# Moving the attention's elementwise work off GpSimd in a hybrid decoder layer

## The chip, the cores and the metric

The kernel runs on one core of a Trainium2 chip. The metric is the device time of one execution in microseconds. A core has TensorE (PE, matmuls, with the weight loads shown as PEld), VectorE (DVE), ScalarE (ACT), GpSimd (POOL) and SyncE (SP, which issues DMAs). Each engine runs its instructions in the order in which they were written to it, and waits on semaphores for the others.

## The reference

One layer, 512 tokens, width 1024, all in float32:

```python
x = x + 0.5 * swiglu(rms_norm(x, n1), gate1, up1, down1)          # width 2816
p = rms_norm(x, nm) @ w_in                                        # z | xBC | dt | q | k | v
y = rms_norm(ssd(conv(xBC), dt) * silu(z))                        # 16 heads of 64, chunks of 128 tokens
q, k = rms_norm(q), rms_norm(k)                                   # 8 heads, 2 parts of 64 each
p1, p2 = softmax(mask(q1 @ k1.T / 8)), softmax(mask(q2 @ k2.T / 8))
o = rms_norm((p1 - lam * p2) @ v) * 0.8                           # per head, width 128
x = x + concat(y, o) @ w_out
x = x + 0.5 * swiglu(rms_norm(x, n2), gate2, up2, down2)
```

## The kernel before, in words

TensorE takes its operands as pairs: a high part rounded to the fast float32 form (fp32r) and a low part, the remainder; a product is three matmuls, high by high, high by low, low by high (`mm3`, lines 168 to 172). So each weight tile, after its DMA into `raw`, is split by `split_part` (lines 124 to 129): a cast to `whi`, by ScalarE (line 128) or, while the flag `pool_hi` is set, by GpSimd (line 126), and a difference `wlo` on VectorE (line 129).

The stages follow one another: first feed-forward, projections with convolution and state-space part, attention, output projection, second feed-forward. The attention is the stage of the change. It runs over eight heads `h`, and in each over four blocks `i` of 128 query tokens, block `i` looking at the first (i+1)*128 keys.

- `qk_proj(h)` projects q and k of one head in two halves of 256 tokens (matmuls of lines 603 to 605, tiles `qk_0` and `qk_1`). It is a filler: a generator that `fill()` advances by one block at a time between other work. It runs about two heads ahead. `qk_half` (line 747) then forms the norm of q and k (lines 749 to 752 and `rsqrt_act`, lines 738 to 742), `qf` and `kf` (757, 759), the casts to `qs` and `kh` on ScalarE (766, 769) and the low parts `qs` and `kl` on GpSimd (767, 770).
- `qk_tr(h)` transposes these on TensorE (788) and copies them out (791 on VectorE for `klT`, 793 on ScalarE).
- `att_s(h, i)` makes the scores `sc` of both parts (808 to 810), their maxima `nmx` (813, 814), the exponentials `pe` with their sums `l` on ScalarE (818), and then p1/l1 - lam*p2/l2: reciprocal (820), a factor (821), the scaling of the first part on GpSimd (822) and the fused difference on VectorE (823).
- `att_t(h, i)` transposes the result (831) and splits it into `atH` (ScalarE, 834) and `atL` (VectorE, 835). `att_av(h)` multiplies by v (845 to 847) and takes squares and a scaled copy on ScalarE (850, 851).
- `att_n(h)` is the head's norm: column sums of the squares `om` (857), `v` = mean plus epsilon (860), `y0` = v ** -0.5 from a logarithm and an exponential (861, 862), and one Newton step, o = o*y0 * (1.5 - 0.5*v*y0*y0), whose products are on GpSimd (864, 866 to 868). `o_split` (893, 894) splits the outcome for the output projection.
- `y_split` (line 873, in head 6) loads the state-space part's output again and splits it: cast on GpSimd (880), difference on VectorE (881). From head 6 on, pieces of the output projection (`wo`, lines 170 to 172) are the fillers.

The loop that sets the program order is at lines 944 to 976. On top of it a scheduler with a timing model of its own reorders the instructions of all engines within what data and buffers allow, when the kernel is built. `pool_hi` is set at line 943 and taken back at line 959, at head 6. There are two PSUM buffers for projections (`J`), four for single banks (`M`) and one for the wide scores (`A`); `qs`, `kh`, `kl` and `pe` have three buffers each.

Of the kernel before, what the change touches and what calls it, by code (L numbers as in the profile page):

```python
# [8 lines left out]
F32 = mybir.dt.float32  # L9
# [4 lines left out]
ALU = mybir.AluOpType  # L14
# [4 lines left out]
P = 128  # L19
# [19 lines left out]
def hymba_layer(ctx: ExitStack, tc: tile.TileContext, xT, gu1, dn1, wxbc, wdt, wz, wv, wqk,  # L39
# [7 lines left out]
    psum = {}  # L47

    def psum_open(**bufs):
        """One set of PSUM pools at a time: A tiles take two banks, M and J tiles one."""  # L50
        for cm, _ in reversed(list(psum.values())):
            cm.__exit__(None, None, None)
        psum.clear()
        for tag, n in bufs.items():
            cm = tc.tile_pool(name=f"ps{tag}", bufs=n, space=PSUM)
            psum[tag] = (cm, cm.__enter__())
# [14 lines left out]
        return psum["P"][1].tile([P, T], F32, tag="P", name=name)  # L71

    def ffn_plan(parts, early):
        """Order of the work: a part's products with w_down run between the next part's with gate and up."""
        plan, downs, f = [], [], 0
        for pi, n in enumerate(parts):
            if pi == 0:
                plan += [("std", e, g) for e in range(n) for g in range(2)]
            else:
                for c in range(n):  # L80
                    if pi == 1 and c == 0:
                        plan += downs[:early]
                        downs = downs[early:]
                    plan.append(("seven", f + c // 2 * 2, c % 2))
                    while downs and len(downs) > KD * (n - 1 - c) // n:
                        plan.append(downs.pop(0))
            downs = [("down", pi, d) for d in range(KD)]
            f += n
        return plan + downs
# [84 lines left out]
    xpool_cm = tc.tile_pool(name="x1", bufs=1, side="right")  # L174
    xpool = xpool_cm.__enter__()
    x1 = [xpool.tile([P, T], F32, name=f"x1_{d}") for d in range(KD)]
    # products of zeros while the first loads run: the tensor engine's clock is up when the data comes
    zeros = const.tile([P, T], BF16, name="zeros")
    V.memset(zeros, 0.0)
    warm = pP("warm")  # L180
# [24 lines left out]
    xnpool = xn_cm.__enter__()  # L205

    def rsqrt(dst, v, shape, tag):
        """dst = v ** -0.5 for small tiles: exponent-halving start and Newton steps."""
        y = tiny.tile(shape, F32, tag=f"rs_y{tag}", name="rs_y")
        t = tiny.tile(shape, F32, tag=f"rs_t{tag}", name="rs_t")  # L210
        ti = t.bitcast(I32)
        V.tensor_scalar(ti, v.bitcast(I32), 1, None, op0=ALU.arith_shift_right)
        V.tensor_scalar(y.bitcast(I32), ti, -1, 0x5F3759DF, op0=ALU.mult, op1=ALU.add)
        for it in range(3):
            V.tensor_mul(t, y, y)
            V.scalar_tensor_tensor(t, t, -0.5, v, op0=ALU.mult, op1=ALU.mult)
            V.scalar_tensor_tensor(dst if it == 2 else y, t, 1.5, y, op0=ALU.add, op1=ALU.mult)

    class Normed:
        """x * w in two parts, and the factors 1/rms(x) by token (columns, and a row on all partitions)."""  # L220

        def __init__(self, pool, sqp, wcol, name):
            self.sqp, self.pool = sqp, pool
# [61 lines left out]
    prep(4)  # L285

    def ffn(xn, x, done, name, parts, early):
        """x += 0.5 * swiglu(xn).

        The 128-column tiles of gate and up in the first part take the products as they are. The others take them in  # L290
        pairs, in Winograd's form of Strassen's product of 2x2 blocks (halves of the contraction, of the tokens
        and the two tiles), seven block products in place of eight, on the normalized tokens.
        """
        sp_cm = tc.tile_pool(name=f"str{name}", bufs=1)
        hp_cm = tc.tile_pool(name=f"ffn{name}", bufs=5)
        sp, hp = sp_cm.__enter__(), hp_cm.__enter__()
# [1 line left out]
        al = sp.tile([P, 4, 7, 256], F32R, name=f"al{name}")  # L298

        def operands(i):  # L300
            # 0: A12, 1: A22, 2: S1, 3: S2, 4: S3, 5: S4, 6: A11, 7: A21
            tx = hp.tile([P, 8, 256], F32, tag="hp", name="tx")
            for k, at in ((i, 6), (i + 4, 0)):
                c = xn.wcol + k
                V.scalar_tensor_tensor(tx[:, at:at + 2, :].rearrange("p a b -> p (a b)"), x[k], col[:, c:c + 1],
                                       xn.rbc, op0=ALU.mult, op1=ALU.mult)
            V.tensor_add(tx[:, 2], tx[:, 7], tx[:, 1])
            V.tensor_sub(tx[:, 3], tx[:, 2], tx[:, 6])
            V.tensor_sub(tx[:, 4], tx[:, 6], tx[:, 7])
            V.tensor_sub(tx[:, 5], tx[:, 0], tx[:, 3])  # L310
            S.copy(ah[:, i], tx[:, 0:7])
            V.tensor_sub(al[:, i], tx[:, 0:7], ah[:, i].bitcast(F32))

        def h_pair(g, u):
            """silu(g) * u in two parts; g and u: the two tiles, [P, 2, T]."""
            h = hp.tile([P, 2, 2, T], F32R, tag="hp", name="h")
            S.activation(g, g, AF.Silu)
            V.tensor_mul(u, u, g)
            S.copy(h[:, 0], u)
            V.tensor_sub(h[:, 1], u, h[:, 0].bitcast(F32))  # L320
            return h
# [6 lines left out]
                PE.matmul(ps, lhsT=lo, rhs=ah[:, i, a], start=False, stop=i == 3)  # L328

        def seven(c, u, nm_):  # L330
            """c[:, f, t] = the pair's two tiles by the two halves of the tokens."""
            w = piece(1)
            q = [pP(f"{nm_}{z}") for z in range(4)]
            half = lambda z, b: q[z][:, b * 256:(b + 1) * 256]
            cc = c.rearrange("p f (t b) -> p f t b", t=2)
            c1, u2, u3, u4 = (u[:, z] for z in range(4))
            product(half(0, 0), 6, w[0], 0)
            product(half(0, 1), 0, w[0], 512)
            S.copy(c1, half(0, 0))
            V.tensor_add(cc[:, 0, 0], half(0, 1), c1)  # L340
            product(half(1, 0), 2, w[1], 0)
            product(half(1, 1), 4, w[1], 512)
            product(half(2, 0), 3, w[2], 0)
            V.tensor_add(u2, half(2, 0), c1)
            V.tensor_add(u3, half(1, 1), u2)
            V.tensor_add(cc[:, 1, 1], half(1, 0), u3)
            V.tensor_add(u4, half(1, 0), u2)
            product(half(2, 1), 1, w[2], 512)
            V.scalar_tensor_tensor(cc[:, 0, 1], half(2, 1), -1.0, u3, op0=ALU.mult, op1=ALU.add)
            product(half(3, 0), 5, w[3], 0)  # L350
            V.tensor_add(cc[:, 1, 0], half(3, 0), u4)
# [56 lines left out]
        hp_cm.__exit__(None, None, None)  # L408
        sp_cm.__exit__(None, None, None)

# [1 line left out]
    xsave = dram.tile([KD, P, T], F32, name="xsave")  # L412
    nm = [None]

# [8 lines left out]
    xpool_cm.__exit__(None, None, None)  # L423
    psum_open(A=2, M=2, J=2)

# [1 line left out]
    mix_cm = tc.tile_pool(name="mix", bufs=1)  # L427
    mix = mix_cm.__enter__()
    row = mix.tile([P, NROW], F32, name="row")
# [158 lines left out]
    V.tensor_scalar(e2, nm.v, EPS, None, op0=ALU.mult)  # L588

    def tok_proj(name, cb, ahead=2):  # L590
        """Projection onto 256 columns by token blocks; yields after each block's matmuls."""
        ws = [piece(ahead), piece(ahead)]
        for half in range(2):
            ps = pJ(f"{name}_{half}")
# [135 lines left out]
            pass  # L730
    last_ssd = lambda: drain_c(8)

# [1 line left out]
    def rsqrt_act(dst, v, shape):  # L734
        """dst = v ** -0.5: exp(-ln(v) / 2) and a Newton step."""
        y = tiny.tile(shape, F32, tag="ra_y", name="ra_y")
        t = tiny.tile(shape, F32, tag="ra_t", name="ra_t")
        S.activation(y, v, AF.Ln)
# [8 lines left out]
    def qk_half(h, half, ps):  # L747
# [16 lines left out]
        kh = at.tile([P, 4, 2, 64], F32R, tag="kh", name="kh", bufs=3)  # L764
        kl = at.tile([P, 4, 2, 64], F32R, tag="kl", name="kl", bufs=3)
        S.copy(qs[:, :, 0, :], qf)
        G.tensor_sub(qs[:, :, 1, :], qf, qs[:, :, 0, :].bitcast(F32))
        kd = kf.unsqueeze(2).to_broadcast([P, 4, 2, 64])
        S.copy(kh, kd)
        G.tensor_tensor(kl, kd, kh.bitcast(F32), op=ALU.subtract)  # L770
        qk[h].append((rs, qs, kh, kl))

    qk = {}
# [25 lines left out]
    def att_s(h, i):  # L799
# [19 lines left out]
                         accum_out=l[:, t:t + 1])  # L819
        V.reciprocal(l, l)  # L820
        V.scalar_tensor_tensor(l[:, 1:2], l[:, 1:2], -1.0, lam, op0=ALU.mult, op1=ALU.mult)
        G.tensor_scalar(pe[:, 0, :K], pe[:, 0, :K], l[:, 0:1], 1.0, op0=ALU.mult, op1=ALU.mult)
        V.scalar_tensor_tensor(pe[:, 0, :K], pe[:, 1, :K], l[:, 1:2], pe[:, 0, :K], op0=ALU.mult, op1=ALU.add)  # L823
        sm[h, i] = pe

# [28 lines left out]
    def att_n(h):  # L854
# [6 lines left out]
        S.activation(y0, v, AF.Ln)  # L861
        S.activation(y0, y0, AF.Exp, scale=-0.5)
        o = oT[:, h, :]
        G.tensor_mul(o, o, y0)
        S.activation(y0, y0, AF.Square)
        G.tensor_mul(v, v, y0)
        G.tensor_scalar(v, v, -0.5, 1.5, op0=ALU.mult, op1=ALU.add)
        G.tensor_mul(o, o, v)

    # output projection pieces that fill the tensor engine while the last head's attention runs  # L870
    yhl = []

    def y_split():
        yh = xnpool.tile([P, KD, T], F32R, tag="xnh", name="yh")
        yl = xnpool.tile([P, KD, T], F32R, tag="xnl", name="yl")
        for t in range(0, KD, 2):
            yt = wpool.tile([P, 1024], F32, tag="raw", name="yt", bufs=3)
            nc.sync.dma_start(yt, ysave[:, t:t + 2].rearrange("p a b c -> p (a b c)"))
            h = yh[:, t:t + 2, :].rearrange("p a b -> p (a b)")
            G.tensor_scalar(h, yt, 1.0, 1.0, op0=ALU.mult, op1=ALU.mult)  # L880
            V.tensor_sub(yl[:, t:t + 2, :].rearrange("p a b -> p (a b)"), yt, h.bitcast(F32))
        yhl.extend((yh, yl))

# [56 lines left out]
    fillers += [qk_proj(h) for h in range(1, 8)]  # L940
    fill()
    fill()
    pool_hi[0] = True
    for h in range(8):
        qk_tr(h)
        fill()
# [9 lines left out]
        prep(taken[0] + 1)  # L956
        fill()
        if h == 6:
            pool_hi[0] = False
            y_split()  # L960
            wo_ps[0], wo_ps[1] = pJ("wo0"), pJ("wo1")
            fillers += wo_fill(0)
# [52 lines left out]
    xn_cm.__exit__(None, None, None)  # L1015
    psum_open(P=8)

# [1 line left out]
    def done2(d):  # L1019
        nc.sync.dma_start(out[d], x2[d])  # L1020

# [62 lines left out]
```

## Time and profile before

| what | value |
|---|---|
| median of three runs | 1207.35 us (1206.51 to 1207.97) |
| span of the profiled execution, first to last instruction | 1203.1 us |
| TensorE busy | 1163.4 us (97%) |
| VectorE busy | 926.0 us (77%) |
| ScalarE busy | 533.8 us (44%) |
| GpSimd busy | 210.6 us (18%) |
| mean granted TensorE clock | 0.990 |

The profile page gives no device time for the profiled execution beside its span; the median of the runs is 4.25 us above it. Busy times are of the union of an engine's instructions. An instruction's duration can overlap that of the next one on the same engine. A matmul's duration is that of its passage through a pipeline, so matmuls overlap and their durations do not add up to TensorE's time.

### The profile page before, as it was taken

What the parts mean: (1) busy time and instruction counts of PE and PEld (TensorE: products, weight loads), DVE (VectorE), ACT (ScalarE), POOL (GpSimd) and SP (SyncE); (2) the same over time, 40 slices, a digit from 0 to 9 for tenths busy, and PEclk for the clock granted to TensorE, in tenths of its full rate; (3) what the DMA queues carried; (4) which work ended last, traced back from release to release, by engine and by line L of the source; (5) the groups of instructions that cost most, each with busy time, mean ns of one, the idle gap of its engine ahead of it and who ended that gap; (6) DMA issues with size and microseconds to landing.
All of it is one profiled execution on the core that took longest, in us unless ns stands there. A gap on an engine that the chain in (4) does not pass through costs nothing.

```text
span 1203.1 us, 19035 instructions
## 1 busy us (share of the span) xinstructions
PE 1163.4 (97%) x7483; PEld 1036.3 (86%) x7483; DVE 926.0 (77%) x1593; ACT 533.8 (44%) x863; POOL 210.6 (18%) x214
## 2 busy tenths in 40 slices
PE   8999999999989999798999998899999999999998
PEld 6889999999967788797998886688789999999997
DVE  6988787787585867989588989636499988787862
ACT  5534343433352355343366675735244443434331
POOL 1000000000031004443255756315100000000000
PEclk9999999999998999899999999999999999999999
DMA  7223333333353224242321102216312333333332
GB/s 231 86 75 97 110 110 97 99 107 88 97 193 114 77 82 140 81 131 73 105 71 36 58 32 76 75 44 209 98 62 89 109 121 100 101 107 102 96 114 83
DMA packets 42393, 119.56 MB, mean 99 GB/s; under 512 B 4608, under 2 KB 9920, under 8 KB 42304
## 3 DMA queue, kind: packets, MB, share of 16 engines
q1 hardware_dynamic: 41024, 114.15, 30.3%
q0 software_dynamic: 1280, 4.20, 1.0%
q8 instruction: 59, 0.97, 0.3%
q14 instruction: 30, 0.25, 0.1%
HBM read 112.00 MB, written 6.32 MB: 98 GB/s over the span
## 4 chain that ended last, share of the span: by engine, by line
PE 40%; DVE 10%; issue 2%; ACT 2%; POOL 1%; DMA 0%; DVEq 0%; ACTq 0%; POOLq 0%
PE s L327 5%; PE s L326 5%; PE s L328 5%; PE dn L170 3%; PE dn L172 3%; PE dn L171 3%; PE wo L170 2%; PE wo L171 2%; PE wo L172 2%; DVE nmx L813 2%; DVE pe L823 1%; PE gu L170 1%; PE gu L172 1%; PE gu L171 1%; DVE wlo L129 1%
## 5 line engine op out<-in xcount | busy, mean ns | idle before, releaser
L129 DVE TENSOR_TENSOR wlo<-raw,whi 128x1024 fp32r<-128x1024 f32 (+3 forms) x225 | 225.9, 1007 | 120.0 <-ACT whi L128 104.4
L128 ACT CAST whi<-raw 128x1024 fp32r<-128x1024 f32 (+2 forms) x204 | 175.7, 865 | 310.2 <-PE s L327 121.7
L327 PE MATMUL s<-al,whi 128*128 128x256 f32 x952 | 265.2, 280 | 0.0
L326 PE MATMUL s<-ah,whi 128*128 128x256 f32 x952 | 263.6, 279 | 0.0
L328 PE MATMUL s<-ah,wlo 128*128 128x256 f32 x952 | 262.6, 279 | 0.0
L327 PEld LDWEIGHTS s<-al,whi 128*128 128x128 f32 x952 | 178.7, 188 | 2.1
L326 PEld LDWEIGHTS s<-ah,whi 128*128 128x128 f32 x952 | 178.5, 188 | 2.0
L328 PEld LDWEIGHTS s<-ah,wlo 128*128 128x128 f32 x952 | 177.2, 187 | 0.1
L170 PE MATMUL dn<-h,whi 128*128 128x512 f32 x352 | 137.6, 394 | 0.0
L172 PE MATMUL dn<-h,wlo 128*128 128x512 f32 x352 | 137.5, 392 | 0.0
L171 PE MATMUL dn<-h,whi 128*128 128x512 f32 x352 | 136.9, 389 | 0.0
L128 ACT CAST whi<-tw 128x1024 fp32r<-128x1024 f32 x68 | 70.3, 1049 | 141.2 <-PE s L327 65.7
L129 DVE TENSOR_TENSOR wlo<-tw,whi 128x1024 fp32r<-128x1024 f32 x68 | 82.1, 1220 | 2.8 <-ACT whi L128 2.5
L172 PEld LDWEIGHTS dn<-h,wlo 128*128 128x128 f32 x352 | 66.1, 188 | 14.6
L171 PEld LDWEIGHTS dn<-h,whi 128*128 128x128 f32 x352 | 66.1, 188 | 12.7
L170 PEld LDWEIGHTS dn<-h,whi 128*128 128x128 f32 x352 | 66.1, 188 | 12.2
L603 PE MATMUL qk<-whi,xhm 128*128 128x256 f32 x256 | 73.3, 287 | 1.1 <-DVE l L820 1.1
L605 PE MATMUL qk<-whi,xlm 128*128 128x256 f32 x256 | 72.8, 285 | 0.0
L604 PE MATMUL qk<-wlo,xhm 128*128 128x256 f32 x256 | 72.7, 284 | 0.0
L362 DVE SCALAR_TENSOR_TENSOR x<-dn,x 128x512 f32<-128x512 f32 x64 | 44.0, 688 | 35.4 <-PE dn L172 34.9
L170 PE MATMUL gu<-xh,whi 128*128 128x512 f32 x160 | 64.9, 406 | 2.7 <-POOL whi L126 1.7
L419 POOL DMA_DIRECT2D xsave<-x x8 | 4.6, 578 | 337.3 <-DVE x L362 337.3
(293 smaller groups left out, 2650.8 us busy)
## 6 DMA issues: line engine op xcount, KB each, us to landing
raw<-in_gu SPq DMA_DIRECT2D x86, 512.0 KB, 3.6
raw<-in_dn SPq DMA_DIRECT2D x48, 384.0 KB, 3.2
raw<-in_wqk SPq DMA_DIRECT2D x16, 512.0 KB, 3.6
raw<-in_wxbc SPq DMA_DIRECT2D x12, 512.0 KB, 3.5
raw<-in_wo SPq DMA_DIRECT2D x10, 512.0 KB, 4.1
raw<-in_dn SPq DMA_DIRECT2D x16, 256.0 KB, 2.7
raw<-in_wz SPq DMA_DIRECT2D x8, 512.0 KB, 3.5
ab<-acs_d SPq DMA_DIRECT2D x8, 512.0 KB, 4.1
```

The lines of the kernel that those rows point to most:

```text
L128: S.copy(hi[:, a:b], raw[:, a:b])
L129: V.tensor_sub(lo[:, a:b], raw[:, a:b], hi[:, a:b].bitcast(F32))
L170: PE.matmul(ps, lhsT=hi, rhs=xh, start=start, stop=False)
L171: PE.matmul(ps, lhsT=hi, rhs=xl, start=False, stop=False)
L172: PE.matmul(ps, lhsT=lo, rhs=xh, start=False, stop=stop)
L326: PE.matmul(ps, lhsT=hi, rhs=ah[:, i, a], start=i == 0, stop=False)
L327: PE.matmul(ps, lhsT=hi, rhs=al[:, i, a], start=False, stop=False)
L328: PE.matmul(ps, lhsT=lo, rhs=ah[:, i, a], start=False, stop=i == 3)
L362: V.scalar_tensor_tensor(x[d], ps, 0.5, x[d], op0=ALU.mult, op1=ALU.add)
L603: PE.matmul(o, lhsT=xh, rhs=hi, start=k == 0, stop=False)
L604: PE.matmul(o, lhsT=xh, rhs=lo, start=False, stop=False)
L605: PE.matmul(o, lhsT=xl, rhs=hi, start=False, stop=k == KD - 1)
```

## The change

In the attention GpSimd's elementwise instructions go to other engines. The low parts of q and k and the scaling of the first softmax part go to VectorE, the casts of the weights (heads 0 to 5) and of y go to ScalarE. The head's norm is written in another way: y0*(1.5 - 0.5*v*y0*y0) is formed first, with two fused instructions on VectorE, and multiplied into o once. Comments were taken out of the file as well, which moves line numbers little: lines 767 to 868 keep theirs.

```diff
@@ qk_half
-        G.tensor_sub(qs[:, :, 1, :], qf, qs[:, :, 0, :].bitcast(F32))
+        V.tensor_sub(qs[:, :, 1, :], qf, qs[:, :, 0, :].bitcast(F32))
...
-        G.tensor_tensor(kl, kd, kh.bitcast(F32), op=ALU.subtract)
+        V.tensor_tensor(kl, kd, kh.bitcast(F32), op=ALU.subtract)
@@ att_s
-        G.tensor_scalar(pe[:, 0, :K], pe[:, 0, :K], l[:, 0:1], 1.0, op0=ALU.mult, op1=ALU.mult)
+        V.tensor_scalar(pe[:, 0, :K], pe[:, 0, :K], l[:, 0:1], None, op0=ALU.mult)
@@ att_n
-        G.tensor_mul(o, o, y0)
-        S.activation(y0, y0, AF.Square)
-        G.tensor_mul(v, v, y0)
-        G.tensor_scalar(v, v, -0.5, 1.5, op0=ALU.mult, op1=ALU.add)
-        G.tensor_mul(o, o, v)
+        t = at.tile([P, T], F32, tag="sq", name="ot")
+        S.activation(t, y0, AF.Square)
+        V.scalar_tensor_tensor(t, t, -0.5, v, op0=ALU.mult, op1=ALU.mult)
+        V.scalar_tensor_tensor(t, t, 1.5, y0, op0=ALU.add, op1=ALU.mult)
+        V.tensor_mul(o, o, t)
@@ y_split
-            G.tensor_scalar(h, yt, 1.0, 1.0, op0=ALU.mult, op1=ALU.mult)
+            S.copy(h, yt)
@@ the loop over heads
-    pool_hi[0] = True
     for h in range(8):
...
         if h == 6:
-            pool_hi[0] = False
             y_split()
```

The scheduler then orders all engines anew. On TensorE, in head 2, before: the transposes of the head's k (khT_6532 and klT_6539, the high and the low part of one of its two halves) with matmuls of head 4's projection (qk_0_6756) between them.

```order
L788 MATMUL khT_6532<-identr,kh 128x128 x4
L605 MATMUL qk_0_6756<-whi,xlm 128x256
L603 MATMUL qk_0_6756<-whi,xhm 128x256
L604 MATMUL qk_0_6756<-wlo,xhm 128x256
L605 MATMUL qk_0_6756<-whi,xlm 128x256
L603 MATMUL qk_0_6756<-whi,xhm 128x256
L604 MATMUL qk_0_6756<-wlo,xhm 128x256
L605 MATMUL qk_0_6756<-whi,xlm 128x256
L603 MATMUL qk_0_6756<-whi,xhm 128x256
L604 MATMUL qk_0_6756<-wlo,xhm 128x256
L605 MATMUL qk_0_6756<-whi,xlm 128x256
L788 MATMUL klT_6539<-identr,kl 128x128 x4
```

The same place on TensorE after the change, up to head 2's scores sc_6719; at_6592 is a transposed softmax tile of head 1.

```order
L788 MATMUL khT_6532<-identr,kh 128x128 x4
L788 MATMUL klT_6539<-identr,kl 128x128 x4
L788 MATMUL qT_6546<-identr,qs 128x128 x4
L788 MATMUL khT_6553<-identr,kh 128x128 x4
L788 MATMUL klT_6560<-identr,kl 128x128 x4
L831 MATMUL at_6592<-ident,pe 128x128 x3
L808 MATMUL sc_6719<-khT,qT 128x384
L809 MATMUL sc_6719<-klT,qT 128x384
```

The projection's matmuls are gone from between; qk_0_6756 starts after head 1's product with v. On VectorE, before: from the maximum of head 1's last scores (sc_6459) to the difference of its two softmax parts (L823).

```order
L813 TENSOR_REDUCE nmx<-sc_6459 128x2
L752 SCALAR_TENSOR_TENSOR qss<-qss,e_4158 128x8
L835 TENSOR_TENSOR atL<-at_6454,atH 128x2x128
L814 TENSOR_TENSOR nmx<-nmx,qrs 128x2
L791 CAST klT<-klT_6539 128x512
L820 RECIPROCAL l<-l 128x2
L740 TENSOR_TENSOR ra_t<-ra_y 128x8
L821 SCALAR_TENSOR_TENSOR l<-l,lam 128x1
L791 CAST klT<-klT_6560 128x512
L741 SCALAR_TENSOR_TENSOR ra_t<-ra_t,qss 128x8
L823 SCALAR_TENSOR_TENSOR pe<-pe,l 128x512
```

The same on VectorE after the change; `ot` and `oT` are head 0's norm.

```order
L813 TENSOR_REDUCE nmx<-sc_6459 128x2
L791 CAST klT<-klT_6539 128x512
L791 CAST klT<-klT_6560 128x512
L814 TENSOR_TENSOR nmx<-nmx,qrs 128x2
L866 SCALAR_TENSOR_TENSOR ot<-ot,ov 128x512
L835 TENSOR_TENSOR atL<-at_6592,atH 128x3x128
L867 SCALAR_TENSOR_TENSOR ot<-ot,osq 128x512
L820 RECIPROCAL l<-l 128x2
L868 TENSOR_TENSOR oT<-oT,ot 128x512
L821 SCALAR_TENSOR_TENSOR l<-l,lam 128x1
L822 TENSOR_SCALAR pe<-pe,l 128x512
L823 SCALAR_TENSOR_TENSOR pe<-pe,l 128x512
```

The norm's three instructions and the scaling now stand in this queue, and the small norm instructions of a projection (L740, L741) are no longer there at this place.

## Rows read from the trace of the kernel before

**Rows 1.** Windows: stretch, length, busy us of each engine (instructions), granted clock, DMA share, GB/s.

```profile
600.00:645.00 45.00, 45.00 (x379) 42.33 (x378) 38.86 (x90) 27.84 (x75) 25.96 (x25) 1.00 0.18 60
645.00:667.70 22.70, 21.32 (x170) 19.27 (x170) 19.64 (x44) 15.14 (x41) 14.84 (x14) 1.00 0.16 47
667.70:690.00 22.30, 22.07 (x182) 20.25 (x180) 20.44 (x43) 16.13 (x43) 15.18 (x15) 1.00 0.16 48
690.00:712.00 22.00, 19.95 (x156) 17.76 (x155) 18.94 (x44) 14.51 (x39) 13.44 (x13) 1.00 0.16 50
712.00:734.00 22.00, 19.94 (x155) 17.39 (x153) 19.35 (x42) 15.67 (x43) 14.06 (x15) 1.00 0.00 1
734.00:760.00 26.00, 23.07 (x118) 18.28 (x119) 23.51 (x37) 14.22 (x33) 12.58 (x11) 1.00 0.47 140
760.00:780.00 20.00, 16.57 (x93) 12.56 (x92) 14.01 (x35) 16.57 (x42) 7.78 (x9) 0.91 0.13 43
```

**Rows 2.** Waits of VectorE, 645 to 734 us: us in total, times, longest.

```profile
DVE l L820 <- ACT pe L818: 6.1, 6, 1.3
DVE pe L823 <- POOL pe L822: 1.7, 4, 0.7
```

**Rows 3.** Timeline of VectorE, 669 to 676 us: start, us, instruction.

```profile
669.05 0.15 DVE L814 TENSOR_TENSOR nmx<-nmx,qrs 128x2 f32<-128x2 f32 x1
669.12 0.68 DVE L791 CAST klT<-klT 128x512 fp32r<-128x512 f32 x1
...
673.38 1.24 DVE L742 SCALAR_TENSOR_TENSOR qrs<-ra_t,ra_y 128x8 f32<-128x8 f32 x1
```

**Rows 4.** Timeline of GpSimd in the same stretch.

```profile
673.05 1.54 POOL L866 TENSOR_TENSOR ov<-ov,osq 128x512 f32<-128x512 f32 x1 [0.28 <-ACT osq L865]
```

**Rows 5.** Lines of VectorE, 592 to 790 us: busy us, mean ns | idle before.

```profile
L823 DVE SCALAR_TENSOR_TENSOR pe<-pe,l 128x256 f32<-128x256 f32 x8 | 9.7, 1206 | 1.1 <-POOL pe L822 0.9
L823 DVE SCALAR_TENSOR_TENSOR pe<-pe,l 128x512 f32<-128x512 f32 x8 | 9.6, 1194 | 2.1 <-POOL pe L822 2.1
L823 DVE SCALAR_TENSOR_TENSOR pe<-pe,l 128x384 f32<-128x384 f32 x8 | 9.4, 1174 | 1.5 <-POOL pe L822 1.5
L821 DVE SCALAR_TENSOR_TENSOR l<-l,lam 128x1 f32<-128x1 f32 x32 | 8.0, 249 | 0.4
...
L742 DVE SCALAR_TENSOR_TENSOR qrs<-ra_t,ra_y 128x8 f32<-128x8 f32 x16 | 7.0, 437 | 0.3
...
L814 DVE TENSOR_TENSOR nmx<-nmx,qrs 128x2 f32<-128x2 f32 x32 | 6.6, 213 | 0.1
...
L752 DVE SCALAR_TENSOR_TENSOR qss<-qss,e 128x8 f32<-128x8 f32 x16 | 6.2, 390 | 0.0
...
L741 DVE SCALAR_TENSOR_TENSOR ra_t<-ra_t,qss 128x8 f32<-128x8 f32 x16 | 5.3, 329 | 0.2
...
L835 DVE TENSOR_TENSOR atL<-at,atH 128x384 fp32r<-128x384 f32 x8 | 4.4, 549 | 0.2 <-ACT atH L834 0.2
...
L740 DVE TENSOR_TENSOR ra_t<-ra_y 128x8 f32<-128x8 f32 x16 | 3.7, 233 | 0.4 <-ACT ra_y L739 0.4
```

**Rows 6.** Lines of VectorE over the whole span, other stages, for prices.

```profile
L387 DVE TENSOR_TENSOR gu<-gu,rbc 128x512 f32<-128x512 f32 x20 | 13.0, 686 | 6.0 <-PE gu L172 6.0
...
L305 DVE SCALAR_TENSOR_TENSOR tx<-x,col,rbc 128x512 f32<-128x512 f32 x16 | 10.8, 748 | 0.0
...
L480 DVE TENSOR_SCALAR a<-u,col 128x512 f32<-128x512 f32 x12 | 6.3, 544 | 2.9 <-ACT xst L487 2.9
...
L310 DVE TENSOR_TENSOR tx<-tx 128x256 f32<-128x256 f32 x8 | 3.0, 424 | 0.0
```

**Rows 7.** Single lines: shortest/median/longest in ns, first and last start.

```profile
L645 DVE TENSOR_SCALAR ab<-ab,acs x64: 269/276/2466, 455.6 to 541.6; 128x128 f32<-128x128 f32 x64
...
L742 DVE SCALAR_TENSOR_TENSOR qrs<-ra_t,ra_y x16: 154/167/1237, 598.3 to 744.3; 128x8 f32<-128x8 f32 x16
```

**Rows 8.** Lines of ScalarE, 592 to 790 us.

```profile
L128 ACT CAST whi<-raw 128x1024 fp32r<-128x1024 f32 x5 | 5.2, 1047 | 8.6 <-DMA raw<-in_wo 6.6 <-PE wo L171 1.8
```

**Rows 9.** Lines of GpSimd, 592 to 790 us.

```profile
L770 POOL TENSOR_TENSOR kl<-kf,kh 128x512 fp32r<-128x512 f32 x16 | 23.4, 1461 | 7.4 <-ACT kh L769 5.1 <-issue 2.3
```

## The prediction

> **What bounds the kernel now.** I read first the windows of the trace around the attention, then the waits of VectorE there, then single instructions of VectorE and GpSimd side by side, and last the prices by line. The first heads keep TensorE full: 45.0 of 45 us. From 645 us on, one head takes about 22.3 us, and TensorE is idle for 1.4, 0.2, 2.1 and 2.1 us of the four stretches, 5.8 us together; in the last two heads it is idle for 2.9 and 3.4 us more [rows 1]. So TensorE is the bound with little room: everything that a better attention can give back is 12.1 us between 645 and 780, and some 1.8 us for the 0.91 of the clock granted in the last stretch. VectorE stands close behind it, busy for 19.6, 20.4, 18.9 and 19.4 us of the same four stretches, mean 19.6; ScalarE has 15.4 and GpSimd 14.4 [rows 1]. What VectorE does not work it waits mainly for the exponentials, 6.1 us, and 1.7 us for GpSimd's scaling of a probability tile [rows 2].
>
> Part of VectorE's busy time is no work. A product of 128x8 elements took 1.24 us from 673.38 us [rows 3], and GpSimd's two-operand product ran from 673.05 to 674.59 us [rows 4]: VectorE's ended when GpSimd's had. The shortest of the same line took 0.154 us [rows 7]. So the two engines hold each other up here, and the change has a gain of its own besides the moved work.
>
> **What the change takes from VectorE.** The extra time by rows, mean less undisturbed price, for eight heads [rows 5 to 7]: the difference of the two softmaxes (L823) 8 x (1.206 - 0.424) + 8 x (1.174 - 0.549) + 8 x (1.194 - 0.748) = 6.3 + 5.0 + 3.6 = 14.8 us. The small ones at 0.15 us each: L821 32 x 0.10, L742 16 x 0.29, L752 16 x 0.24, L741 16 x 0.18, L814 32 x 0.06, L740 16 x 0.08 = 3.2 + 4.6 + 3.8 + 2.9 + 1.9 + 1.3 = 17.7 us. Together 32.5 us, 4.1 us a head. Not all need come back: some may have been idle time otherwise. I take all of it.
>
> **What it adds to VectorE.** qs: 16 x 0.424 = 6.8 us. kl: 16 x 0.686 = 11.0 us. The scaling of the probabilities (L822), 128 to 512 columns: the rows of two other products with a column show 0.276 and 0.544 us for the ends [rows 6, 7], 0.37 and 0.45 us between them, 1.64 us a head, 13.1 us (from both sides: not below the 0.15 us of a tiny instruction, 4.8 us in all, and not above the 0.69 us of a two-operand one at full width, 22 us). The norm: two fused instructions at 0.748 and a product at 0.686, 2.18 us a head, 17.5 us. Sum 48.4 us, 6.1 us a head. Instructions that follow at once overlap: one started at 669.05 for 0.15 us and the next at 669.12 [rows 3], some 0.08 us of overlap, so the 11 new ones of a head cost 0.9 us less: 5.2 us. Net on VectorE: +1.1 us a head (with the overlap uncounted +2.0; with L822 at its low end about 0).
>
> Of the scaling the rows show 0.544 us at 512 columns, against 0.686 us for a two-operand product [rows 6]. The Trainium skill (VectorE: DVE Perf Modes, section The perf-mode tier table) lets a float32 product with a column run at twice the rate of a two-operand one, 1227 against 2293 ns at 2048 columns. The row does not reach that factor. By the page the widest scaling would be 0.37 us, an estimate as 0.686 x 1227 / 2293, all of them 8.9 us in place of 13.1, and the net 0.5 us a head smaller; I keep the row.
>
> **What it adds to ScalarE.** 13 weight casts leave GpSimd, two to a head at 1.05 us [rows 8], and four casts of y in head 6: ScalarE goes from 15.4 to 17.5 us a head, still under VectorE and TensorE; I cost it at nothing as long as the exponentials don't queue behind the casts (a rival below). In the last two heads the weight casts were on ScalarE already.
>
> **What the new order does.** VectorE at 19.6 + 1.1 = 20.7 us, with the 2.6 us a head that it still has to stand idle (22.2 less 19.6), makes a head of 23.3 us in place of 22.2, since nothing in the change takes the wait for the exponentials away. The 1.7 us of waits for GpSimd in four heads go, 0.4 us a head, so I take +0.8 us a head. For five heads (1 to 5) that is +4 us. Head 0 has slack on VectorE (38.9 of 45 us in the first stretch, [rows 1]), and the last two heads have projections of the output to run beside them; there I take nothing, with -6 to +6 us.
>
> Once, a stretch comes without filler. In the order before, as its rows on TensorE show, the transposes of head 2 stand between matmuls of a projection. In the order after, from the last product of head 0's attention to that of head 1's no projection matmul stands on TensorE; the two halves of head 3's projection have already run. Behind the last scores of head 1 (sc_6459) TensorE has 45 matmuls of its own; at 22.3 us for 170 to 182 of them [rows 1], 0.13 us each, that is 5.9 us. VectorE in the same place has 19 instructions from the maximum of sc_6459 to the low part of tile 3: nine of 512 columns (three fused ones at 0.748, six at 0.686), 6.4 us; the maximum over 1024, 1.3 us; 0.55 us for 384 columns, 0.54 us for the scaling, 0.85 us for two of 256 columns, 0.9 us for the tiny ones: 10.5 us, less 18 x 0.08 us of overlap, 9.1 us. TensorE waits for the end of it, as its next product reads that low part: 3.2 us, and with one wait for the exponentials of about 1 us, 4 us.
>
> **The sum.** +4 (five heads) + 4 (the stretch without filler) + 0 (the last two heads) = +8 us. The profiled execution spans 1203.1 us; the median of the runs is 1207.35 us, 4.25 us above the span, which is what lies around it and the spread between executions. Neither is changed by the edit, so I add to the median: 1215 us.
>
> **Rivals.** First, faster: VectorE, freed, keeps ahead of TensorE, and the shorter chains (two hand-overs to GpSimd fewer for each probability tile) let the idle time of TensorE shrink. For it speak the 1.24 us product and the 1.2 us differences [rows 3, 5], and that the order is written by a scheduler which sees instructions undisturbed. It decides if the added work overlaps so well that VectorE has under 19.6 us a head. It gives back at most the 12.1 us of idle time; about 7 of it, 1200 us. Against it: the moved work by rows is larger than what is freed.
> The Trainium skill (GPSIMD Engine Reference, section Elementwise, side-by-side cycle accounting) has VectorE about twice as fast as GpSimd on two-operand work; the rows agree (kl takes 1.46 us on GpSimd [rows 9], and 0.69 us is the price here), and a reader who goes by it alone would forecast this rival.
>
> Second, no difference: the +1.1 us and the two hand-overs cancel, and the stretch without filler is made up in the last heads, where TensorE is idle for 6.4 us: 1207 us.
>
> Third, much slower: ScalarE's queue decides. Two casts of 1.05 us a head stand ahead of exponentials and of the copies that VectorE waits for; if each delays the chain fully in the six heads that get them, 12.6 us come on top of the 4 us of the stretch without filler: 1224 us. Against it: ScalarE has 6.8 us a head free.
>
> **How the numbers follow.** What a measurement of this kernel can tell from no change is about 0.2%, 2.4 us. The forecast, +8 us, has a chance of 0.40; faster 0.27; no difference 0.18; much slower 0.15. So faster 0.27, same 0.18, slower 0.55. Cases of both signs hold much of the chance: the likeliest one's own range is 1210 to 1221 us. The range that should hold 8 times in 10 goes to the faster rival's middle at the low end, 1200, and to the much slower one at the high end, 1224.
>
> **What would show it.** Right: in the profile after, L823 at 0.35 to 0.75 us and L742 near 0.17 us; VectorE busy for over 20 us of a head; TensorE idle for 3 us or more in head 1 or 2, just ahead of its product with V; the period of a head at 23 us. Wrong: a period at or under 22 us, or VectorE under 19.5 us a head (then the moved work is cheaper than its rows say), or long waits of VectorE for ScalarE's casts, which would be the third rival.

## The result, and the profile after

The changed kernel takes 1214.86 us, the median of 4 runs (1213.43 to 1216.13); the kernel before, run beside it, 1206.93 us (1206.06 to 1207.97). The ratio is 1.0065, with a 95% interval of 1.0051 to 1.0079: slower by 8 us. The profiled execution spans 1211.7 us, 8.6 us more than before, at a mean granted clock of 0.982 against 0.990 (the profiled execution of before is a quick one, see below the table of all runs). GpSimd's busy time falls from 210.6 to 90.9 us.

The windows of after around the attention, in the columns of [rows 1].

```profile
600.00:645.00 45.00, 43.47 (x363) 39.67 (x361) 36.39 (x95) 31.36 (x75) 0.00 (x0) 1.00 0.22 71
645.00:667.70 22.70, 19.10 (x127) 16.96 (x128) 18.65 (x55) 15.81 (x41) 0.00 (x0) 0.85 0.00 1
667.70:690.00 22.30, 19.47 (x141) 17.54 (x140) 19.19 (x53) 16.62 (x41) 0.00 (x0) 0.92 0.15 48
690.00:712.00 22.00, 22.00 (x181) 20.48 (x180) 18.62 (x53) 17.59 (x43) 0.00 (x0) 1.00 0.15 48
712.00:734.00 22.00, 20.03 (x156) 17.61 (x155) 19.30 (x53) 16.98 (x43) 0.00 (x0) 1.00 0.08 25
734.00:760.00 26.00, 18.79 (x119) 15.92 (x118) 23.52 (x57) 20.07 (x46) 0.00 (x0) 0.76 0.34 112
760.00:780.00 20.00, 20.00 (x114) 16.28 (x113) 12.94 (x23) 9.94 (x20) 0.00 (x0) 0.96 0.14 40
```

VectorE has more instructions (55, 53, 53, 53 against 44, 43, 44, 42 in the four stretches from 645 us) and is busy for 18.9 us of a stretch on average, against 19.6. That does not mean less work: the stretches are fixed times, and a slower kernel gets less done in each. From the first transposes of q and k (L788) to the second feed-forward, where both kernels have the same stage to do, VectorE is busy for 3.1 us more, and stands idle for 5.6 us more (before, then after):

```profile
598.80:854.40 255.60, 242.66 (x1578) 208.64 (x1577) 190.43 (x373) 152.31 (x360) 129.52 (x124) 0.99 0.25 78
598.70:863.10 264.40, 246.39 (x1570) 212.41 (x1568) 193.64 (x457) 168.18 (x373) 14.50 (x14) 0.95 0.23 75
```

Of TensorE's idle time after, 3.6, 2.8 and 7.2 us lie in three stretches (645 to 667.7, 667.7 to 690, 734 to 760), and in these the granted clock is 0.85, 0.92 and 0.76; the 0.96 of the last stretch is the end of the same time at half clock. Before, it was 1.00 everywhere but in the last stretch.

Lines of VectorE after, 592 to 790 us, that answer to [rows 5]:

```profile
L770 DVE TENSOR_TENSOR kl<-kf,kh 128x512 fp32r<-128x512 f32 x16 | 11.0, 687 | 1.3 <-ACT kh L769 1.1
L767 DVE TENSOR_TENSOR qs<-qf,qs 128x256 fp32r<-128x256 f32 x16 | 6.7, 419 | 0.0
L823 DVE SCALAR_TENSOR_TENSOR pe<-pe,l 128x512 f32<-128x512 f32 x7 | 5.2, 749 | 0.2
...
L867 DVE SCALAR_TENSOR_TENSOR ot<-ot,osq 128x512 f32<-128x512 f32 x7 | 4.8, 689 | 0.1
...
L823 DVE SCALAR_TENSOR_TENSOR pe<-pe,l 128x256 f32<-128x256 f32 x8 | 3.9, 484 | 0.1
L822 DVE TENSOR_SCALAR pe<-pe,l 128x512 f32<-128x512 f32 x7 | 3.4, 479 | 0.0
...
L742 DVE SCALAR_TENSOR_TENSOR qrs<-ra_t,ra_y 128x8 f32<-128x8 f32 x16 | 2.6, 164 | 0.2
```

With no GpSimd instruction from 645 to 780 us the hold-ups are gone: L823 at 256 columns takes 484 ns where it took 1206, L742 164 where it took 437.

What TensorE waits for after, 590 to 780 us (total, times, longest):

```profile
PE o L846 <- DVE atL L835: 5.8, 3, 2.8
PE at L831 <- ACT osq L850: 3.4, 1, 3.4
PE sc L808 <- ACT pe L818: 2.9, 1, 2.9
```

Before, the longest single wait there was this one:

```profile
PE at L831 <- DVE l L821: 1.8, 1, 1.8
```

Now the first of the three places on TensorE's timeline (start, duration, what ended the idle time before it):

```profile
647.72 0.44 PE L808 MATMUL sc<-khT,qT 128*128 128x384 f32 x1 [2.90 <-ACT pe L818]
...
649.76 1.11 PE L831 MATMUL at<-ident,pe 128*128 128x128 f32 x4 [0.88 <-DVE pe L823]
...
653.77 0.63 PE L846 MATMUL o<-atL,vh 128*128 128x512 f32 x1
654.20 0.63 PE L847 MATMUL o<-atH,vl 128*128 128x512 f32 x1
```

The wide scores wait for the one PSUM buffer `A`, which head 1's exponentials still read. There is no projection matmul to run meanwhile. Behind the wait matmuls of 512 columns start 0.43 us apart (653.77 and 654.20) where they start 0.23 us apart at full rate: the clock is at its 1.2 GHz level for 6.8 us. The second place is the product of head 2 with v, on TensorE and then on VectorE:

```profile
675.05 0.49 PE L845 MATMUL o<-atH,vh 128*128 128x512 f32 x1
678.36 0.50 PE L846 MATMUL o<-atL,vh 128*128 128x512 f32 x1 [2.83 <-DVE atL L835]
```

```profile
673.42 1.22 DVE L129 TENSOR_TENSOR wlo<-raw,whi 128x1024 fp32r<-128x1024 f32 x1
...
674.63 1.22 DVE L129 TENSOR_TENSOR wlo<-raw,whi 128x1024 fp32r<-128x1024 f32 x1
675.77 0.42 DVE L813 TENSOR_REDUCE nmx<-sc 128x2 f32<-128x256 f32 x1
676.10 0.68 DVE L751 TENSOR_REDUCE qss<-sqk 128x8 f32<-128x512 f32 x1
676.70 0.42 DVE L767 TENSOR_TENSOR qs<-qf,qs 128x256 fp32r<-128x256 f32 x1
677.03 0.68 DVE L813 TENSOR_REDUCE nmx<-sc 128x2 f32<-128x512 f32 x1
677.63 0.68 DVE L835 TENSOR_TENSOR atL<-at,atH 128x512 fp32r<-128x512 f32 x1
```

VectorE never pauses, but the one instruction that TensorE needs, L835, stands behind a weight split, the projection's norm (L751, L767) and two maxima. `atH` of this tile was written by 675.0 us. In the order of its queue VectorE first serves work that TensorE does not need yet.

The third place is heads 5 and 6, where ScalarE, too, has its queue in the wrong order:

```profile
746.07 0.22 ACT L739 ACTIVATE ra_y<-ra_y 128x8 f32<-128x8 f32 x1
748.40 1.05 ACT L880 CAST yh<-yt 128x1024 fp32r<-128x1024 f32 x1 [2.11 <-DMA yt<-ysave]
...
754.41 0.62 ACT L128 CAST whi<-raw 128x512 fp32r<-128x512 f32 x1 [1.01 <-DMA raw<-in_wo]
754.94 0.61 ACT L893 CAST oh<-oT 128x512 fp32r<-128x512 f32 x1
755.46 0.59 ACT L850 ACTIVATE osq<-o 128x512 f32<-128x512 f32 x1
```

ScalarE stands 2.11 us for the load of a y tile and 1.01 us for a weight; the squares L850, for which TensorE waits 3.4 us, come after; the product that they read had ended by 752.8 us.

### The profile page after: what moved, and what is told of

Same layout as the page of the kernel before. It is cut to its first block, busy times and chain, and to the rows that moved or that the text cites. A ratio compares the mean times of both kernels' runs of the same rounds, so it can differ in the third digit from the quotient of the medians.

```text
span 1211.7 us, 18948 instructions
## 1 busy us (share of the span) xinstructions
PE 1168.3 (96%) x7483; PEld 1040.7 (86%) x7483; DVE 928.9 (77%) x1681; ACT 553.5 (46%) x880; POOL 90.9 (8%) x101
## 4 chain that ended last, share of the span: by engine, by line
PE 50%; DVE 3%; ACT 2%; issue 0%; DMA 0%
PE s L327 5%; PE s L326 5%; PE s L328 5%; PE dn L170 3%; PE dn L172 3%; PE dn L171 3%; PE wo L170 2%; PE wo L171 2%; PE wo L172 2%; PE qk L603 2%; PE qk L604 2%; PE qk L605 2%; PE gu L170 1%; PE gu L172 1%; PE gu L171 1%; PE sc L808 1%
## 5 line engine op out<-in xcount | busy, mean ns | idle before, releaser
L128 ACT CAST whi<-raw 128x1024 fp32r<-128x1024 f32 (+2 forms) x217 | 190.0, 879 | 303.4 <-PE s L327 121.7
L129 DVE TENSOR_TENSOR wlo<-raw,whi 128x1024 fp32r<-128x1024 f32 (+3 forms) x225 | 222.6, 992 | 114.5 <-ACT whi L128 108.6
L172 PE MATMUL dn<-h,wlo 128*128 128x512 f32 x352 | 137.5, 392 | 0.0
L129 DVE TENSOR_TENSOR wlo<-tw,whi 128x1024 fp32r<-128x1024 f32 x68 | 82.0, 1220 | 3.1 <-ACT whi L128 3.0
L172 PEld LDWEIGHTS dn<-h,wlo 128*128 128x128 f32 x352 | 66.1, 188 | 14.6
L172 PE MATMUL gu<-xh,wlo 128*128 128x512 f32 x160 | 63.0, 394 | 0.0
```

What stands on the lines that cost most here:

```text
L128: S.copy(hi[:, a:b], raw[:, a:b])
L129: V.tensor_sub(lo[:, a:b], raw[:, a:b], hi[:, a:b].bitcast(F32))
L172: PE.matmul(ps, lhsT=lo, rhs=xh, start=False, stop=stop)
```

## The experiments

Each of the 12 was timed in five rounds beside the kernel before, in three sets; the kernel before had 1207.1, 1206.4 and 1207.4 us in them. Four ideas were under test. VectorE theory: its added work lengthens each head (the prediction's step of +4 us for five heads). Buffer theory: the norm's new tile `ot` shares the single buffer "sq" with the squares of q and k, and this ties the norm to the projections. Order theory: TensorE waits where the new order leaves no projection matmuls between those of the attention, whatever engine has how much work. ScalarE theory: its casts stand ahead of exponentials and squares.

**Buffer alone, on the kernel before.** No work moves; the square of the norm only goes to the shared buffer.

```diff
-        S.activation(y0, y0, AF.Square)
-        G.tensor_mul(v, v, y0)
+        t = at.tile([P, T], F32, tag="sq", name="ot")
+        S.activation(t, y0, AF.Square)
+        G.tensor_mul(v, v, t)
```

> The kernel before with one thing changed: the square in the head's norm is written to a tile of its own name in the buffer 'sq', of which there is one and in which the squares of the projections' norms stand as well, as in the changed kernel. No instruction moves to another engine. Theory BUFFER (the changed norm's new tile makes a projection's first step wait for the norm of a head, so TensorE runs out of projection matmuls): a run of about 67 matmuls without filler in head 2, slower than before by 4 to 10 us. Theory VECTORE (on record: the added work on VectorE makes a head longer): the same time as before, within 2 us.

Measured 1217.38 us, ratio 1.0086 (1.0072 to 1.0099): 10 us slower for a buffer, at the top of buffer theory's range. TensorE idles 8.3 of 22.7 us and gets a clock of 0.76 in one stretch of that kernel:

```profile
645.00:667.70 22.70, 14.38 (x64) 11.01 (x63) 16.88 (x42) 15.18 (x41) 13.78 (x16) 0.76 0.07 23
```

So the buffer is enough by itself. Is it needed?

**The changed kernel with the norm in place**, without the shared buffer, in four VectorE instructions:

```diff
-        t = at.tile([P, T], F32, tag="sq", name="ot")
-        S.activation(t, y0, AF.Square)
-        V.scalar_tensor_tensor(t, t, -0.5, v, op0=ALU.mult, op1=ALU.mult)
-        V.scalar_tensor_tensor(t, t, 1.5, y0, op0=ALU.add, op1=ALU.mult)
-        V.tensor_mul(o, o, t)
+        V.scalar_tensor_tensor(v, v, -0.5, y0, op0=ALU.mult, op1=ALU.mult)
+        V.tensor_mul(v, v, y0)
+        V.scalar_tensor_tensor(v, v, 1.5, y0, op0=ALU.add, op1=ALU.mult)
+        V.tensor_mul(o, o, v)
```

> The changed kernel with the norm in place in four VectorE instructions, without the tile in 'sq': one VectorE instruction of 0.69 us more a head, one ScalarE square less. Theory BUFFER: the run without filler in head 2 goes and 5 to 7 us of the 8 come back (1207 to 1210 us), if no new run takes its place. Theory VECTORE: 8 x 0.69 us more work on VectorE, up to 5 us slower than the changed kernel (1215 to 1220 us).

Measured 1215.45 us, ratio 1.007 (1.0058 to 1.0082): no gain: outside buffer theory's range, and at the low end of VectorE theory's. Other long waits stand in the place of those removed. **The changed kernel with the old norm on GpSimd** (the norm's part of the change undone, the shared buffer gone with it):

> The changed kernel with the norm as before, on GpSimd and without the tile in the shared buffer; all else stays on VectorE and ScalarE. Theory BUFFER: no run without filler in head 2 (29 matmuls at most before head 7, 112 in head 7): 1207 to 1211 us. Theory VECTORE and SCALARE: a little under the changed kernel by the 17.5 us of norm work that VectorE is spared, 1211 to 1214 us.

Measured 1215.92 us, ratio 1.0077 (1.0062 to 1.0093), above both ranges, with VectorE spared the norm. TensorE waits three times as in the first place above, scores for exponentials:

```profile
PE sc L808 <- ACT pe L818: 7.4, 3, 4.2
```

The buffer is sufficient on the order before, and not needed in the order after: buffer theory fails as the cause.

**The changed kernel with the y casts back on GpSimd** (`G.tensor_scalar` in place of `S.copy` in `y_split`):

> The changed kernel with the four casts of y back on GpSimd. Theory SCALARE (in head 6 the casts of y stand in ScalarE's queue ahead of the copies that TensorE waits for, 9 us of idle time between 744 and 758 us): 3 to 7 us less than the changed kernel, 1208 to 1212 us. Theory BUFFER alone or VECTORE: no more than 1 us less.

Measured 1214.22 us, ratio 1.0067 (1.0054 to 1.008): no gain, which ScalarE theory misses. The wait of 3.4 us for the squares L850 is gone, but another of 4.3 us has come:

```profile
PE wo L170 <- DVE l L820: 4.3, 1, 4.3
```

**With the weight casts back** (`pool_hi` set as before):

> The changed kernel with the weight casts of heads 0 to 5 back on GpSimd (13 casts). Theory SCALARE in its recorded form (two casts a head delay the chain, up to 12 us): 4 to 12 us less than the changed kernel. Theory BUFFER: no gain, the run without filler stays (84 matmuls in head 2), within 2 us of 1215. Theory VECTORE: slightly slower than the changed kernel, as GpSimd's casts hold VectorE up again.

Measured 1217.77 us, ratio 1.0091 (1.0074 to 1.0107); the interval overlaps that of the changed kernel. Taking ScalarE's new work away doesn't help in either case: ScalarE theory has no support, though single waits behind its casts are seen above. The wait for the squares L850 is still there in the last run, 2.9 us.

**One part alone on the kernel before.** Scaling (L822) on VectorE:

```diff
-        G.tensor_scalar(pe[:, 0, :K], pe[:, 0, :K], l[:, 0:1], 1.0, op0=ALU.mult, op1=ALU.mult)
+        V.tensor_scalar(pe[:, 0, :K], pe[:, 0, :K], l[:, 0:1], None, op0=ALU.mult)
```

> The kernel before with only the scaling of the first softmax part moved to VectorE (32 instructions). Theory INTERLEAVE (what counts is whether matmuls of projections still stand between the attention's on TensorE, else it waits for over 2 us at a time and its granted clock falls behind that): the order keeps them between the transposes of every head, so within 3 us of before, 1204 to 1210 us, and at most one stretch at half clock between 590 and 790 us. Theory VECTORE: +0.5 to 1 us a head, 1211 to 1215 us.

Measured 1209.52 us, ratio 1.0023 (1.0011 to 1.0036): in the range of order theory (here INTERLEAVE), but not by its sign, as there are four stretches at half clock between 590 and 790 us in place of at most one. The low parts of q and k (L767, L770) on VectorE, `G.` to `V.` in both lines:

> The kernel before with only the low parts of q and k moved to VectorE (32 instructions). Theory INTERLEAVE: as for the scaling, 1204 to 1210 us, but for head 7, in which the order has a run of 106 matmuls without filler where before has 75: up to 3 us more. Theory VECTORE: 17.8 us of added work, less some of GpSimd's hold on VectorE, 1209 to 1215 us.

Measured 1202.86 us, ratio 0.9971 (0.996 to 0.9982): faster than before, and below both ranges. The norm alone on VectorE, in place as above:

> The kernel before with only the head's norm moved to VectorE, in place in four instructions, without a tile in the shared buffer. Theory INTERLEAVE and BUFFER: projections stay between the transposes in heads 1 to 5, a run of 109 without filler in head 7 instead of 75: 1205 to 1211 us. Theory VECTORE: 22.9 us of added work less what GpSimd's 40 us of two-operand products held up: 1207 to 1214 us.

Measured 1205.87 us, ratio 0.9994 (0.9982 to 1.0006): no difference, in order theory's range and below VectorE theory's. The weight casts alone on ScalarE (the two lines with `pool_hi` left out):

> The kernel before with the 13 weight casts of the attention on ScalarE alone. ScalarE theory: 13 x 1.05 us, 13.6 us more on ScalarE in 180 us, of which a third delays exponentials or squares, 1210 to 1213 us. Order theory: 1204 to 1211 us, and where it lies follows the waits over 2 us and the time at half clock between 590 and 790 (under 7 us of it: 1207 or less; 14 us or more: 1210 or more).

Measured 1202.94 us, ratio 0.9963 (0.9947 to 0.9979): faster, a little below order theory's range, with 6.8 us at half clock. The y casts alone on ScalarE:

> The kernel before with the four y casts of heads 6 and 7 on ScalarE alone (four of 1.0 us instead of GpSimd's). ScalarE theory (they stand ahead of squares and exponentials of head 6): a wait of TensorE of 2 us or more between 740 and 765 with half clock behind it, 1209 to 1213 us. Order theory without it: no such wait, 1205 to 1208 us.

Measured 1203.42 us, ratio 0.9963 (0.9949 to 0.9976): faster than both expectations, and no wait of 2 us between 740 and 765. Of five parts alone, three make the kernel faster by 0.3 to 0.4%, one does nothing, one costs 0.2%. The norm as the change writes it, with `ot` in the shared buffer, was not tried alone.

**Two good parts together**, q and k low parts and the norm in place:

> The kernel before with the low parts of q and k on VectorE and the Newton step on VectorE in place (four instructions); scale, weight casts and y casts stay on GpSimd. Order theory (each part alone costs little; the time is set by how many waits of 2 us or more TensorE gets): alone they gave 1202.9 and 1205.9 us, so about 1202 us if the two add, and 1200 to 1208 us since the order is drawn up anew, with under 10 us at half clock between 590 and 790. VectorE theory (its work lengthens each head): 4 x 0.69 us and 2 x (0.42 + 0.69) us more on VectorE, 5 us per head, less the hold-ups; 1209 to 1215 us.

Measured 1217.43 us, ratio 1.0084 (1.0071 to 1.0097). Both expectations missed: alone they were 3.6 us faster and equal, together they are 10 us slower. The effects do not add. The whole stage, first of q and k alone, then of q and k with the norm, then of before with the shared buffer, then of the changed kernel with the old norm:

```profile
597.90:850.30 252.40, 242.34 (x1573) 208.46 (x1571) 187.78 (x399) 153.39 (x358) 94.91 (x93) 0.99 0.25 78
598.40:866.90 268.50, 248.63 (x1572) 214.58 (x1570) 196.94 (x431) 149.10 (x350) 54.95 (x61) 0.95 0.23 73
598.40:866.00 267.60, 250.30 (x1580) 215.63 (x1579) 186.07 (x374) 154.31 (x361) 125.63 (x124) 0.96 0.23 74
600.00:863.80 263.80, 246.00 (x1570) 210.87 (x1568) 189.41 (x434) 167.19 (x373) 53.49 (x46) 0.96 0.23 75
```

Within the pair VectorE has 9 us more to do in the slow one, and that alone would speak for VectorE theory. It falls by the other two: VectorE is busy there for 186 and 189 us, less than the 190 before, and the stage is 12 and 8 us longer; while the norm in place alone, with 196 us, costs nothing. So VectorE's load does not set the time. What q and k with the norm has is long waits, 590 to 780 us:

```profile
PE at L831 <- DVE pe L823: 6.7, 2, 4.7
PE sc L808 <- ACT pe L818: 4.3, 3, 2.4
PE om L857 <- ACT osq L850: 2.0, 1, 2.0
```

**Is it the clock?** The changed kernel in its own order, instruction for instruction, with 15 products with zeros on TensorE inside four of its waits:

```diff
-    osqs = {}
+    osqs = {}; pad = lambda po, n, a=False, z=False: [PE.matmul(po, lhsT=zeros[:, :P], rhs=zeros, start=a and j == 0, stop=z and j == n - 1) for j in range(n)]
...
-            PE.matmul(po[:, n0:], rhs=atH[:, kb, n0:], start=kb == 0, stop=False, **st)
+            pad(po, 4 * (h == 5 and kb == 0), a=True); PE.matmul(po[:, n0:], rhs=atH[:, kb, n0:], start=kb == 0 and h != 5, stop=False, **st); pad(po, 4 * (h in (2, 5) and kb == 0))
...
-                      stop=kb == NB - 1)
+                      stop=kb == NB - 1 and h != 5); pad(po, 3 * (h == 5 and kb == NB - 1), z=True)
```

> The changed kernel with its order kept instruction for instruction, and 15 products with a tile of zeros put on TensorE where it waits: four between L845 and L846 in head 2 (the wait of 2.83 us at 675), four ahead of L845 and four behind it in head 5 (waits of 1.24 and 2.59 us at 745 to 749), three behind the last L847 of head 5 (3.38 us at 752). They add zero to o. Clock theory (what the change costs is mostly the half clock that follows these waits): the stretches at 679.5 (3.4 us) and 747.8 (13.7 us) go or shrink; half of their 17.1 us is 8.5 us at most, so 1207 to 1212 us. Wait theory (the waits themselves are the cost): the fifteen take 3.5 us of TensorE inside waits of 10 us, nothing else moves, 1214 to 1216 us.

Measured 1215.61 us, ratio 1.0071 (1.0055 to 1.0087): wait theory's time. In head 5 the zeros did keep the clock up, from the product with v to the wait behind it:

```profile
749.11 1.04 PE L837 MATMUL o<-zeros 128*128 128x512 bf16 x4
751.86 0.50 PE L846 MATMUL o<-atL,vh 128*128 128x512 f32 x1 [1.72 <-DVE atL L835]
752.20 0.39 PE L847 MATMUL o<-atH,vl 128*128 128x512 f32 x1
...
758.33 0.45 PE L831 MATMUL at<-ident,pe 128*128 128x128 f32 x1 [3.82 <-ACT osq L850]
```

The same L847 in the changed kernel:

```profile
749.91 0.63 PE L847 MATMUL o<-atH,vl 128*128 128x512 f32 x1
```

It takes 0.39 us with the zeros and 0.63 without, and time at half clock falls from 23.9 to 17.1 us. But the product only ends sooner, and TensorE then waits 3.82 us for the squares instead of 3.38: ScalarE's queue decides that time. In head 2 the stretch of 3.4 us stayed. So half clock in front of this longer wait cost nothing. Clock theory is not settled by it: the zeros took away 6.8 us of the 23.9, all in front of this wait or in it, and what half clock costs in a stretch with nothing to wait for behind it was not tried by itself.

**All runs in one table.** From each profiled execution: the time from the first transposition of q and k (L788) to the first matmul of the second feed-forward, TensorE's idle time in it, its waits of 1.5 us and more, the time at half clock, and for how long VectorE is busy.

| kernel | ratio | stage, us | idle, us | long waits, us (count) | half clock, us | VectorE busy, us |
|---|---|---|---|---|---|---|
| q, k alone | 0.9971 | 252.4 | 10.1 | 4.7 (2) | 6.8 | 187.7 |
| weight casts alone | 0.9963 | 253.1 | 10.5 | 4.0 (2) | 6.8 | 178.4 |
| y casts alone | 0.9963 | 254.5 | 11.1 | 2.0 (1) | 3.4 | 187.6 |
| before | 1 | 255.7 | 13.0 | 3.5 (2) | 3.4 | 190.5 |
| norm in place alone | 0.9994 | 256.8 | 11.1 | 4.5 (2) | 13.7 | 196.5 |
| scaling alone | 1.0023 | 261.5 | 14.6 | 5.7 (3) | 13.7 | 199.7 |
| after, norm in place | 1.007 | 263.3 | 15.8 | 8.9 (4) | 20.5 | 198.6 |
| after, y casts back | 1.0067 | 263.3 | 17.8 | 12.1 (4) | 17.1 | 195.3 |
| after, old norm | 1.0077 | 263.7 | 17.8 | 13.0 (5) | 20.5 | 189.4 |
| after | 1.0065 | 264.4 | 18.0 | 11.7 (4) | 23.9 | 193.6 |
| after, zeros in waits | 1.0071 | 264.4 | 15.8 | 10.4 (4) | 17.1 | 193.6 |
| before, shared buffer | 1.0086 | 267.5 | 17.3 | 9.3 (3) | 23.9 | 186.0 |
| after, weight casts back | 1.0091 | 267.7 | 19.3 | 12.5 (5) | 27.3 | 199.2 |
| q, k and norm in place | 1.0084 | 268.6 | 19.9 | 11.1 (4) | 27.3 | 197.0 |

All the difference arises in this stage (8.7 us, of 8.6 in the span). Under 6 us of long waits the stage takes 252 to 262 us, from 8.9 us on 263 to 269. A straight line through idle time plus half of the half-clock time fits the 14 stages with a slope of 0.73 and no residual over 2.4 us; a slope under 1 would fit that some of either is hidden behind something else, which was not tried.

Each row is one execution. Their times lie between 2.0 us below (q, k alone) and 3.2 us above (after, weight casts back) the median of their kernel. That of before spanned 1203.1 us at a granted clock of 0.990; its 51 timed runs in the three sets spanned 1205.0 us at the median, at clocks of 0.984 to 0.989 and once 0.991. These 51 runs, all of one order, tell something of the clock: the 13 at 0.984 spanned 1206.5 us on average, the 17 at 0.987 1204.1 us. So 0.003 of the clock, 3.6 us of the span, went with 2.4 us of time. After ran at 0.980 on average and before at 0.986, which is 7 us of the span; at that price some 5 of the 8 us go with the clock, an estimate. Waits and clock come together in these runs, and none of them parts the two.

Order theory in its recorded form, by the length of stretches without filler, does not come out of the traces either. The fastest kernel has a stretch of 108 matmuls without filler in head 7 (before 77). The changed kernel with the old norm has none of 40 or more before head 7 and still has waits of 4.2, 2.2 and 1.8 us there. And in some kernels the matmul that waits is itself a filler whose operand comes late, as in scaling alone a matmul of L172 that waits 2.3 us for `wlo` (L129). What is left standing is the wider form: an order alone, with no work moved, can cost 10 us (the shared buffer), and no part that was tried alone costs more than about 3 us. What makes an order good or bad was not isolated; no run put projection matmuls back into the places where the changed kernel waits.

## Why the prediction was right in time and half wrong in its reasons

- *TensorE is the bound, with 12.1 us to give back.* Right: in the table the stage's length goes with TensorE's idle time and its time at half clock.
- *VectorE loses hold-ups and gains work.* The terms hold. The seven lines of the sum came out 30.7 us shorter in all (32.5 forecast), the new instructions at 46.4 us (48.4 forecast: L767 6.7, L770 11.0, L822 12.2, the norm 16.5). Not in the sum were the splits of weights and of y (L129, L881), some 4 us shorter. Over the stage VectorE is busy for 3.1 us more, 0.4 a head, where 1.1 a head were forecast; the splits are most of the difference.
- *So a head takes 0.8 us more, +4 us over five heads.* This step failed. It kept VectorE's idle time as it was (2.6 us a head) and charged all that its work grows to TensorE; 1.1 less 0.4 is also 0.7 and not 0.8. In the stage VectorE's work grew by 3.1 us, and its idle time, which was to shrink a little, by 5.6 us: it did not hold TensorE up by being full, but by the place of single instructions in its queue and in ScalarE's. From 690 to 712 us TensorE has no idle time at all with VectorE at 18.6 us. Of the marks that I had set, the period of 23 us is met, but says little: from the first transposes of head 1 to those of head 6 (618.1 to 733.9 us) a head takes 23.2 us, and before (617.7 to 731.9) 22.8. VectorE over 20 us of a head is not met: 19.5 in the same time, before 20.1.
- *A stretch without filler in head 2, +4 us.* Right in place and size of the wait: 2.90 + 0.88 us of idle time between the products of heads 0 and 1. The releaser was another (the exponentials of head 1's last scores, through PSUM buffer `A`, not a low part), and the 6.8 us at half clock behind it was not in the sum. Nor did I look for more such stretches: heads 2 and 5 have long waits as well (2.83, 2.59 and 3.38 us).
- *The last two heads at 0.* In the idle time nearly so: 7.2 us from 734 to 780, against 6.4. In the clock not: 13.7 us of half clock against 3.4.
- *ScalarE's casts at nothing.* Right: alone both sets make the kernel faster, and putting them back gains nothing that lies outside the intervals. But in the changed kernel the squares do queue behind casts in head 5, 3.4 us for TensorE, and without the casts of y another wait takes that place.
- *First rival, faster.* Its deciding point (VectorE under 19.6 us a head) was met, narrowly, with 19.5, and the time still went the other way. I had given it the wrong condition: the load of VectorE does not decide.

The 8 us thus came out of one right term of 4 and a wrong term of 4, which stood in for two more places with long waits and for the time at half clock. That they came to the same 4 is luck. Why this scheduler's orders get long waits with several parts moved, or with the shared buffer alone, and few with any one part alone, is not settled.

## What to carry to other kernels

Where an order is drawn up by a scheduler at build time, an edit is priced by the order that it leaves behind: look on the engine that bounds the stage for all places where it waits, and price the wait and the slower clock behind it; the length of a stretch without independent work is not the price. Load per engine said little here, where no engine but the bound was full: in two kernels about 10 us slower than before VectorE had less to do. Compare loads over the same work: in a window of fixed length an engine looks less busy in a slower kernel. Try the parts of such a change one by one before dropping or keeping it whole: three of five parts alone beat both kernels (q and k 1202.86, weight casts 1202.94, y casts 1203.42 us), and two harmless ones together cost 10 us.

## What the runs showed of the hardware

- VectorE instructions took several times as long beside GpSimd's work (1.24 us for 128x8 elements beside a two-operand product, [rows 3, 4]), and were short where GpSimd ran nothing: 1206 to 484 ns (L823, 256 columns), 437 to 164 ns (L742, 128x8).
- A fused instruction with a constant took 0.686 to 0.689 us at 512 columns, with a column operand 0.749 us; the scaling by a column 0.479 us.
- In the kernel after TensorE's granted clock was at its 1.2 GHz level for 6.8 us from 648.8 us on, 1.1 us after a wait of 2.90 us had ended, with matmuls of 512 columns 0.43 instead of 0.23 us apart. In head 5 four zero products, 1.04 us, on each side of the first matmul of a product, with a wait of 1.72 us behind them, kept it at its full level through that product; in head 2 four behind the first matmul alone, with a wait of 1.96 us, did not.
